# A gated delta rule with U times values and U times keys made ahead of the chunk scan

## The chip, the cores and the metric

One core of a Trainium2 chip runs the whole kernel. The metric is the device time of one execution in microseconds (us). Each core has five engines that run their own instruction lists in order and wait for each other by semaphores: TensorE (PE in the profile; its weight loads are PEld), VectorE (DVE), ScalarE (ACT), GpSimd (POOL) and SyncE (SP), whose list is a queue of DMA transfers. PSUM is the memory that TensorE writes, in banks of 128 partitions by 512 float32.

## The reference

One block of a decoder: 1024 tokens of width 1024 are normalised and projected; two mixers run side by side, each output is gated and projected up, the two are merged by sigmoid gates, and an output projection, a residual add and a last normalisation follow. Mixer A is a dilated window attention. Mixer B, which the change touches, is a gated delta rule with 8 heads of 64 keys by 64 values, computed in 16 chunks of 64 tokens:

```python
a = jnp.einsum('bhnid,bhnjd->bhnij', k_beta, kc) * decay_strict
t_inv = lax.linalg.triangular_solve(eye + a, ...)
u = t_inv @ (vc * bc[..., None])
w = t_inv @ (k_beta * jnp.exp(G)[..., None])
attn = jnp.einsum('bhnid,bhnjd->bhnij', qc, kc) * decay_incl
...
def step(state, inp):
    q_e, at, u_c, w_c, k_d, dec = inp
    v_new = u_c - jnp.einsum('bhck,bhkv->bhcv', w_c, state)
    o = jnp.einsum('bhck,bhkv->bhcv', q_e, state) + jnp.einsum('bhij,bhjv->bhiv', at, v_new)
    state = state * dec[..., None, None] + jnp.einsum('bhck,bhcv->bhkv', k_d, v_new)
    return state, o
```

`t_inv` (called U in the kernel, up to scalings by beta and by the norm of the keys) can be applied to values and keys for all chunks at once, as the reference does, or inside the scan to their difference, since u − w·S = t_inv·(beta·v − beta·exp(G)·(k·S)).

## The kernel before

Almost all of TensorE's time goes to projections. They are made in float16 with high and low parts: a *tick* is three matmuls of 128x512 (lines 171 to 173: high·high, high·low, low·high). A *unit* is 32 ticks, or 28 where a Strassen-like form with seven products is used; the 796 ticks of the units from the keys of mixer B on are handed out by an object called the Feed. TensorE's order is written by hand: the code of the mixers runs in program order, and wherever a step depends on another engine it calls `feed.tick(n)` to put n ticks of projection between; `feed.until(name)` runs ticks until a unit is done, and `feed.later(n, fn)` calls fn after n more ticks. The order on the other engines is made by a scheduler by priorities, and each engine, SyncE's queue too, then keeps that order. PSUM has tags of banks: three banks for projections, two each for G and S, one for O.

The order of the units is: the end of the attention's projections, then keys, values (two halves of four heads each), gates 3 and 4, queries, gate 5, z units a and b, gates 6 and 7, up-projections. Between them stand, in this order:

- `pg` (lines 1065 to 1076): sums of the log decays over chunks, by small matmuls from `gx` and `bg`, with exponentials on ScalarE; five ticks stand ahead of it, and the attention of its last set of heads runs behind it.
- `decay(hb)` for a half hb of the heads (lines 1126 to 1141): a tile `gm` is made on VectorE for each of 8 token tiles and multiplied by a mask of ones; two ticks are given to the first tile.
- `keys_side` (1190): sums of squares, k·k products (`pairs`, line 1181, 4 runs of 32 matmuls of 64x64, in all four quadrants of the array), and `spill_keys`, which multiplies keys from PSUM by a decay and writes `kd` to DRAM. `solve` (1221) inverts 32x32 blocks on VectorE.
- `values` (1299): after the conv of values, two `turn`s transpose them (line 1306), VectorE multiplies by beta into `rv`, and `rv` goes to DRAM. The second turn stands three ticks behind the first.
- `merge(hb)` (1246): joins the 32x32 blocks to U by `left` and `right` (1265 and 1280), with five ticks between its three stages; U is then written to DRAM.
- `pairs(hb, qT, ...)`: the masked q·k products, written to DRAM.

The chunk scan (from line 1454) goes over 8 token tiles of two chunks each. A chunk has three runs of dependent matmuls of 64x64, each float32 matmul showing as two instructions in the trace:

1. k·S and q·S (line 1485, 16 matmuls). VectorE makes z = rv − bgk·(k·S) by two multiplies of 128x128 and two subtractions of 64x256. Ticks: 4.
2. U·z (line 1506, 8 matmuls). VectorE multiplies by rk to `vn`. Ticks: 2.
3. kdec·vn (line 1515, 8 matmuls). VectorE adds to the state S (`Sb`). Ticks: 2.

After the two chunks of a tile comes at·vn (line 1526, 16 matmuls). The tick counts are PACE = (4, 2, 2).

Of the kernel before, what the change touches and what calls it, by code (L numbers as in the profile page):

```python
# [10 lines left out]
F32 = mybir.dt.float32  # L11
# [7 lines left out]
S = 1024  # L19
# [34 lines left out]
PACE = (4, 2, 2)  # L54
# [12 lines left out]
def hybrid_block(ctx: ExitStack, tc: tile.TileContext, A):  # L67
# [991 lines left out]
    feed.tick(5)  # L1059
    pg = bank("G", 2)  # L1060
# [3 lines left out]
    for h2 in range(2):  # L1064
        PE.matmul(pg[64 * h2:64 * h2 + 64, 128:192], lhsT=ones[:, 0:64],
                  rhs=gx.rearrange("p t c (q e) -> p (t c) q e", e=2)[:, :, :, h2],
                  start=True, stop=True, skip_group_check=True)
# [5 lines left out]
    SC.copy(hi4, pg[:, 192:256].rearrange("p (a t h) -> p a t h", a=2, t=8))
    ggf = gg.rearrange("p t h -> p (t h)")
    PE.matmul(pg[:, 0:64], lhsT=upto, rhs=ggf, start=False, stop=True, skip_group_check=True)
# [651 lines left out]
```

## Time and profile before

| | us |
|---|---|
| runs | 1113.74, 1116.79, 1113.9 |
| median | 1113.9 |
| the profiled execution | 1113.02 |
| its span | 1111.2 |
| TensorE busy | 1069.2 |
| VectorE busy | 843.8 |
| ScalarE busy | 545.6 |
| the scan lies between about | 790 and 912 |

The span runs from the first instruction to the last; 1.8 us lie around it. A row of a group of instructions gives line, engine, operation, output and inputs by name, size, count, then busy time and the mean in ns of one, then the idle time of the engine just before such instructions with the engine and line that ended it. Rows of the timeline give a start, a duration and the instructions joined in it. Matmuls overlap: the step from one start to the next tells what one costs, not its duration.

### The profile page before, as it was taken

To read this page: it belongs to the slowest core of one execution; us is meant where nothing else is said; L and a number is where in the kernel's file an instruction comes from. 1 tells how busy PE (TensorE), PEld (TensorE's weight loads), DVE (VectorE), ACT (ScalarE), POOL (GpSimd) and SP (SyncE) were. 2 spreads that over 40 slices of the span, in tenths; PEclk is the share of its full clock that TensorE was granted. 3 is DMA by queue.
4 is the path that set the end of the run, shared out by engine and by line. 5 is a ranking of instruction groups with operands and counts; after the bars stand their busy time and mean duration, and the time that the engine had idled before them with its cause. 6 is when DMAs were issued, how large, how long until landed. Compare 5 with 4: busy or idle time off the path is not lost.

```text
span 1111.2 us, 23274 instructions
## 1 busy us (share of the span) xinstructions
PE 1069.2 (96%) x9230; PEld 646.3 (58%) x9230; DVE 843.8 (76%) x1970; ACT 545.6 (49%) x1218; POOL 57.5 (5%) x103
## 2 busy tenths in 40 slices
PE   6999999999999999989989999999999999999997
PEld 6894685765957755856545544455455554444444
DVE  5798988879879689969955996975788777775223
ACT  6455766666666656457634523243543345331211
POOL 1200000000000000000010000000000000110000
PEclk9999999999999999999999999999999999999999
DMA  8144522623517233631234346373654444662221
GB/s 288 58 109 120 135 75 68 167 66 114 127 49 179 80 101 90 168 102 45 72 106 125 116 128 176 108 211 142 195 163 120 123 153 147 243 206 77 78 95 57
DMA packets 91709, 138.33 MB, mean 124 GB/s; under 512 B 30784, under 2 KB 57792, under 8 KB 90704
## 3 DMA queue, kind: packets, MB, share of 16 engines
q1 hardware_dynamic: 70368, 86.12, 26.3%
q0 software_dynamic: 12128, 44.11, 12.7%
q10 hardware_dynamic: 9104, 6.62, 1.9%
q8 instruction: 72, 1.18, 0.5%
q14 instruction: 37, 0.30, 0.1%
HBM read 85.24 MB, written 32.70 MB: 106 GB/s over the span
## 4 chain that ended last, share of the span: by engine, by line
PE 55%; DVE 30%; ACT 8%; issue 3%; DMA 3%; SPq 0%; ACTq 0%; DVEq 0%
PE ps_mm L171 14%; PE ps_mm L173 14%; PE ps_mm L172 14%; DVE rt L75 3%; DVE wlo L72 3%; ACT sm L770 2%; DVE ca L72 2%; DVE tl L75 2%; DVE sm L766 2%; DVE ro L75 2%; DVE pcAl L75 1%; PE ps_S L172 1%; PE ps_S L171 1%; PE ps_S L173 1%; DVE pcBl L75 1%
## 5 line engine op out<-in xcount | busy, mean ns | idle before, releaser
L173 PE MATMUL ps_mm<-h_hi,wlo 128*128 128x512 f16 (+1 forms) x552 | 208.8, 378 | 0.8 <-DVE wlo L72 0.8
L172 PE MATMUL ps_mm<-h_lo,whi 128*128 128x512 f16 (+1 forms) x492 | 186.0, 378 | 0.8 <-DVE h_lo L75 0.8
L171 PE MATMUL ps_mm<-h_hi,whi 128*128 128x512 f16 (+1 forms) x492 | 186.5, 379 | 0.0
L173 PEld LDWEIGHTS <-wlo 128*128 128x128 f16 x788 | 77.4, 98 | 89.4 <-issue 2.7
L172 PEld LDWEIGHTS <-whi 128*128 128x128 f16 x848 | 83.3, 98 | 70.5 <-issue 5.8
L171 PEld LDWEIGHTS <-whi 128*128 128x128 f16 x848 | 83.2, 98 | 69.9 <-issue 1.1
L171 PE MATMUL ps_mm<-whi,h_hi 128*128 128x256 f16 x384 | 105.1, 274 | 0.0
L173 PE MATMUL ps_mm<-whi,h_lo 128*128 128x256 f16 x384 | 104.7, 273 | 0.0
L172 PE MATMUL ps_mm<-wlo,h_hi 128*128 128x256 f16 x384 | 104.7, 273 | 0.0
L770 ACT ACTIVATE sm<-sm,osb 128x128 f32<-128x128 f32 (+1 forms) x160 | 69.6, 436 | 56.7 <-DVE osb L766 53.6
L72 DVE SCALAR_TENSOR_TENSOR wlo<-wstage,whi 128x1024 f16<-128x1024 f32 x50 | 60.9, 1219 | 13.4 <-ACT whi L154 13.2
L75 DVE TENSOR_TENSOR tl<-ps_G,th 128x256 f16<-128x256 f32 (+1 forms) x96 | 51.9, 541 | 20.9 <-ACT th L785 20.8
L766 DVE CUSTOM_DVE_ANT_0 sm<-ps_S,amask 128x128 f32<-128x128 f32 (+1 forms) x192 | 59.2, 346 | 8.3 <-PE ps_S L759 8.2
L75 DVE TENSOR_TENSOR rt<-rx,tabs 128x512 f32<-128x512 f32 x96 | 64.4, 686 | 1.4 <-ACT rx L576 0.4
L72 DVE SCALAR_TENSOR_TENSOR ca<-xc,cw,ca 128x512 f32<-128x512 f32 x72 | 53.6, 745 | 4.5 <-ACT ca L992 3.6
L780 PE MATMUL ps_G<-cons,sm 128*128 128x128 f32 x280 | 48.4, 276 | 4.9 <-ACT sm L770 2.3
L154 ACT ACTIVATE whi<-wstage 128x1024 f16<-128x1024 f32 x49 | 51.5, 1051 | 0.9 <-DMA wstage<-in_w 0.8
L171 PE MATMUL ps_mm<-wo,mhi 128*128 128x512 f16 (+2 forms) x136 | 49.5, 366 | 0.0
L172 PE MATMUL ps_mm<-wo,mhi 128*128 128x512 f16 (+2 forms) x136 | 49.5, 366 | 0.0
L173 PE MATMUL ps_mm<-wo,mlo 128*128 128x512 f16 (+2 forms) x136 | 49.4, 366 | 0.0
L780 PEld LDWEIGHTS ps_G<-cons,sm 128*128 128x128 f32 x280 | 35.5, 141 | 22.4 <-ACT sm L770 6.0
L172 PEld LDWEIGHTS <-h_hi 128*128 128x128 f16 x384 | 45.8, 119 | 1.7
(324 smaller groups left out, 2526.2 us busy)
## 6 DMA issues: line engine op xcount, KB each, us to landing
wstage<-in_w POOLq DMA_DIRECT2D x68, 512.0 KB, 5.0
og<-osb ACTq DMA_DIRECT2D x32, 132.0 KB, 2.3
og<-og SPq DMA_DIRECT2D x32, 132.0 KB, 2.2
gspa<-gst SPq DMA_DIRECT2D x16, 256.0 KB, 2.0
gspb<-gst SPq DMA_DIRECT2D x16, 256.0 KB, 3.3
sga<-gspa SPq DMA_DIRECT2D x8, 512.0 KB, 5.1
wstage<-in_w_up POOLq DMA_DIRECT2D x8, 512.0 KB, 5.1
sgb<-gspb SPq DMA_DIRECT2D x8, 512.0 KB, 5.9
```

The source lines that it names most:

```text
L72: (eng or V).scalar_tensor_tensor(out, in0, scalar, in1, op0=op0, op1=op1)
L75: (eng or V).tensor_tensor(out, in0, in1, op)
L154: in_turn(SC.activation(hi[:, 4 * c:4 * c + 4], st, AF.Copy, scale=W_SCALE))
L171: PE.matmul(out, lhsT=wh(k), rhs=mh(k), start=first and i == 0, stop=False, skip_group_check=True)
L172: PE.matmul(out, lhsT=wh(k), rhs=ml(k), start=False, stop=False, skip_group_check=True)
L173: last_pe[0] = PE.matmul(out, lhsT=wl(k), rhs=mh(k), start=False, stop=last and i == len(ks) - 1, skip_group_check=True).ins.name
L766: V.tensor_tensor_reduce(P[:, u, :128 * nk], psc[:, u * 256:u * 256 + 128 * nk], mask, -cexp, -NEG, ALU.add, ALU.min, accum_out=osb[:, 256 ...
L770: SC.activation(P[:, u, :128 * nk], P[:, u, :128 * nk], AF.Exp, bias=osb[:, 256 + hd:257 + hd], scale=-1.0, accum_out=osb[:, 260 + hd:261 ...
L780: PE.transpose(pt[:, c:c + 128], P[:, u, i * 128:i * 128 + 128], ident)
```

## The change

- A new generator `state_parts(hb)` runs ten ticks (`UW_LAG[1]`) after `merge(hb)`: for each group of four token tiles it reads `rv` and the keys times beta and decay (`kb`) back from DRAM, makes u = U·rv and w = kb·U by 64 matmuls of 64x64 (a batch) into two G and two S banks, has ScalarE copy the four banks into tiles `uw` (tag rv, three buffers) and writes them to DRAM by six transfers. Between the two batches of a half stand 14 ticks in half 0 (`UW_LAG[0] + UW_LAG[2]`) and 6 in half 1.
- The scan reads u, w, q, kd and at from DRAM and has two runs a chunk: w·S and q·S, with two subtractions vn = u − w·S of 128x128 behind it, and kdec·vn. Ticks: PACE = (3, 3). The loads of U and rv in the scan, the multiply by rk and the scaling by bgk are gone; beta and rk are folded into U by one multiply of 128x1024 in `solve`.
- `keep_keys` has ScalarE copy the keys from PSUM, and `spill_keys`, now after `pairs`, makes kd and kb of them by two multiplies of 128x1024 a group and writes both to DRAM.
- `pg` with its matmuls is put into `over_chunks`, which `feed.later` calls after 20 ticks; the five ticks ahead of it are gone. The first two `gm` tiles take the place of a tile `x7`. The second turn of values stands six ticks behind the first. Gate 6 goes ahead of the z units, behind gate 5.
- DRAM tensors between stages: kd, rv, kb, u, w, a and q (2 MB each, written and read), where there were kd, rv, U, a and q.

```diff
-PACE = (4, 2, 2)
+PACE = (3, 3)
+UW_LAG = (8, 10, 6)
...
-AT = 1
+V_GAP = 6
+GM_LAG = 2
+PG_LAG = 20
+PAIR_TICKS = 4
...
-    feed.tick(5)
-    pg = bank("G", 2)
...
+    def over_chunks():
+        pg = bank("G", 2)
...
+    feed.later(PG_LAG, over_chunks)
     feed.tick(ATT_LEAD)
     feed.run(att_run(*sets[-1], tiles[sets[-1]], ATT_PACE_LAST))
...
-            gm = p2_.tile([128, 2, 2, 64], F32, name="gm", tag="gm", bufs=2)
+            if hb == 0 and t < 2:
+                if t == 0:
+                    room = wst.tile([128, 512], F32, name="x7", tag="x7", bufs=1)
+                gm = room[:, 256 * t:256 * t + 256].rearrange("p (e q i) -> p e q i", e=2, q=2)
+            else:
+                gm = p2_.tile([128, 2, 2, 64], F32, name="gm", tag="gm", bufs=2)
...
+    def spill_keys(hb):
+        hs = slice(4 * hb, 4 * hb + 4)
+        for g in range(2):
+            ts = slice(4 * g, 4 * g + 4)
+            k = key_rows(hb, g)
+            kd = p2_.tile([128, 4, 4, 64], F32, name="kd", tag="T1p", bufs=1)
+            TT(kd, k, bc(eGl[:, ts, hs], 64), ALU.mult)
+            nc.sync.dma_start(out=kd_d[ts, :, hs].rearrange("t p h c -> p t h c"), in_=kd)
+            TT(k, k, bc(bgk[:, ts, hs], 64), ALU.mult)
+            nc.sync.dma_start(out=kb_d[hb][:, ts], in_=k)
...
+        TT(X, X, bsc[:, 1, None, :].to_broadcast([128, 32, 32]), ALU.mult)
...
+    def state_parts(hb):
+        def load(g):
+            ts = slice(4 * g, 4 * g + 4)
+            rv = p2_.tile([128, 4, 4, 64], F32, name="rvt", tag="vT", bufs=2)
+            tag = ("As", "X")[g] if hb else "vT"
+            kb = p2_.tile([128, 4, 4, 64], F32, name="kbt", tag=tag, bufs=1 if hb else 2)
+            nc.sync.dma_start(out=rv, in_=rv_d[ts, :, 4 * hb:4 * hb + 4].rearrange("t p h v -> p t h v"))
+            nc.sync.dma_start(out=kb, in_=kb_d[hb][:, ts])
+            return rv, kb
+        loads = [load(g) for g in range(1 + hb)]
+        yield
+        for g in range(2):
+            if g and not hb:
+                loads.append(load(g))
+                feed.tick(UW_LAG[0])
+            rv, kb = loads[g]
+            pu, pw = [[bank(n, 2), bank(n, 2)] for n in "GS"]
+            for n in range(8):
...
+                            PE.matmul(pu[r][b:b + 64, o:o + 64], lhsT=Ub, rhs=rv[rs, t, 2 * q + e], ...)
...
+                            PE.matmul(pw[r][b:b + 64, o:o + 64], lhsT=kb[rs, t, 2 * q + e], rhs=Ub, ...)
+            for x, ps2 in enumerate((pu, pw)):
+                for r in range(2):
+                    uw = p2_.tile([128, 4, 2, 64], F32, name="uw", tag="rv", bufs=3)
+                    with tc.high_priority():
+                        SC.copy(uw, ps2[r].rearrange("p (t q i) -> p t q i", q=2, i=64))
...
+            yield
...
-            feed.later(V_LAG + 3, lambda: turn(4))
+            feed.later(V_LAG + V_GAP, lambda: turn(4))
...
+    def state_side(hb):
+        parts = state_parts(hb)
+        next(parts)
+        merge(hb, *solved[hb], packs[hb])
+        feed.tick(UW_LAG[1])
+        for _ in parts:
+            feed.tick(UW_LAG[2])
...
-                with tc.high_priority():
-                    for e in range(2):
-                        TT(z[:, e::2], hv(pkq[e][:, :128]), bc(bv[:, e::2], 64), ALU.mult)
-                    for hb in range(2):
-                        r = rows(c2 ^ hb)
-                        TT(z[r], rvt[r, 4 * hb:4 * hb + 4], z[r], ALU.subtract)
+                        TT(vn[:, c2, e], un[:, c2, e], hv(pwq[e][:, :128]), ALU.subtract)
...
-            pvn = bank("O", 1)
-            for n, (hb, j) in enumerate(order):
-                PE.matmul(pvn[r, j * 64:j * 64 + 64], lhsT=U[r, hb, j % 2, j // 2], rhs=z[r, j], ...)
-            with tc.high_priority():
-                TT(vn[:, c2], hv(pvn[:, :256]), bc(rks[:, t, c2], 64), ALU.mult)
-            feed.tick(PACE[1])
```

Three places show how the instructions stand. The first is SyncE's queue around the merging of half 0. Before, the last `rv` is written and then U (u_d0) goes out:

```order
L1312 DMA rv_d_8145<-rv_9461 128x4x128 [waits DMAHW2_49,DVE_49]
L1418 DMA u_d0_8147<-MT0_8136 128x1024 [waits DMAHW5_49,DMAHW3_49,Activation_49]
L1418 DMA u_d0_8147<-MT0_8136 128x1024 [waits DMAHW4_49,Activation_49]
L912 DMA gspb1_9597<-gst_9598 128x512 [waits Activation_49]
L912 DMA gspb1_9597<-gst_9626 128x512 [waits DMAHW6_49,Activation_49]
L1242 DMA u_d1_9087<-X_8989 128x1024 [waits DMAHW7_49,DVE_49,Pool_49]
```

After, the loads for the second batch (rvt, kbt) stand around the six writes of the first:

```order
L916 DMA gspb1_9600<-gst_9629 128x512 [waits DMAHW6_49,Activation_49]
L1328 DMA rvt_9737<-rv_d_8126 128x4x256 [waits DMAHW7_49,PE_49]
L1365 DMA un_d_8130<-uw_9700 64x4x128 [waits DMAHW0_49,Activation_49]
L1365 DMA un_d_8130<-uw_9700 64x4x128 [waits DMAHW1_49]
L1365 DMA un_d_8130<-uw_9704 64x4x128 [waits DMAHW2_49,Activation_49]
L1365 DMA un_d_8130<-uw_9704 64x4x128 [waits DMAHW3_49]
L1362 DMA wn_d_8131<-uw_9708 128x4x128 [waits DMAHW4_49,Activation_49]
L1362 DMA wn_d_8131<-uw_9711 128x4x128 [waits DMAHW5_49,Activation_49]
L1329 DMA kbt_9738<-kb_d0_8132 128x1024 [waits DMAHW6_49,PE_49]
```

The writes of U are gone from the queue, and the second load of keys is its seventh transfer after the load of values.

The second place is ScalarE behind the merging of half 1. Before, its two last copies into U (MT1) are followed by a gate's eviction (gst), a scaling of squares in PSUM and a weight piece:

```order
L1287 COPY MT1_8138<-ps_O_10185 32x16x32 [waits PE_49]
L1287 COPY MT1_8138<-ps_O_10185 32x16x32
L911 ACTIVATE gst_10317<-ps_mm_10178 128x512 [waits DMAHW6_49,PE_49,Activation_49]
L1167 ACTIVATE ps_S_10329<-ps_S_10329 128x512 [waits PE_49]
L318 ACTIVATE whi_10349<-wstage_10074 128x512 [waits DMASW1_49]
```

After, the evictions of the batches stand there, four for the first batch, and the first of the second:

```order
L322 ACTIVATE whi_10515<-wstage_10253 128x512 [waits DVE_49]
L1360 COPY uw_10501<-ps_G_10433 128x512 [waits DMAHW5_49,PE_49]
L1360 COPY uw_10505<-ps_G_10434 128x512 [waits DMAHW3_49,DMAHW2_49,PE_49]
L1360 COPY uw_10509<-ps_S_10435 128x512 [waits DMAHW4_49,PE_49]
L915 ACTIVATE gst_10534<-ps_mm_10420 128x512 [waits DMAHW2_49,PE_49,Activation_49]
L1360 COPY uw_10512<-ps_S_10436 128x512 [waits DMAHW4_49,DMAHW3_49,Activation_49]
L1360 COPY uw_10612<-ps_G_10544 128x512 [waits DMAHW5_49,DMAHW6_49,PE_49,Activation_49]
```

A gate's eviction stands ahead of the fourth, and the copies wait for DMA queues, the writes of tiles that had the same buffers.

The third place is TensorE behind the last projection of gates, at the sums over chunks. Before, after a transposing product of the attention's outputs (osb) a last tick comes, and then `pg`:

```order
L866 MATMUL ps_G<-cons,osb 128x128 x2
L171 LDWEIGHTS whi
L171 MATMUL ps_mm<-h_hi,whi 128x512
L172 LDWEIGHTS whi
L172 MATMUL ps_mm<-h_lo,whi 128x512
L173 LDWEIGHTS wlo
L173 MATMUL ps_mm<-h_hi,wlo 128x512
L1065 MATMUL ps_G<-gx,cons 64x64 x2
L1071 MATMUL ps_G<-bg,cons 64x64 x2
L1075 MATMUL ps_G<-bg,cons 128x64
L1076 MATMUL ps_G<-bg,cons 128x64
```

After, the scores of the last attention set (Ks by Qh and Ql) follow there:

```order
L870 MATMUL ps_G<-cons,osb 128x128 x2
L761 LDWEIGHTS Qh
L761 MATMUL ps_S<-Ks,Qh 128x128
L763 LDWEIGHTS Ql
L763 MATMUL ps_S<-Ks,Ql 128x128
```

The four rows of `pg` now come sixteen ticks later, between ticks, as L1070, L1076, L1080 and L1081.

More of the change, by code (lines that the diff above doesn't have):

```diff
@@ L1435, in hybrid_block @@
         pairs(hb, qT, E[hb])
-        spill(1, hb, E)
+        spill(hb)
         sumsq(hb, qT, rq[:, :, 4 * hb:4 * hb + 4])
-    feed.until(("gate", 5))
+    feed.until(("gate", 6))
     gctx.close()
@@ L1457, in hybrid_block @@
             by_chunk(rqs, rq)
-        rvt = cp.tile([128, 8, 64], F32, name="rvt", tag="rvt", bufs=2)
-        nc.sync.dma_start(out=rvt, in_=rv_d[t])
-        U = cp.tile([128, 2, 2, 2, 64], F32, name="U", tag="U", bufs=2)
-        at = cp.tile([128, 2, 2, 2, 64], F32, name="at", tag="at", bufs=AT)
+        un = cp.tile([128, 2, 2, 2, 64], F32, name="un", tag="un", bufs=2)
+        wt = cp.tile([128, 2, 4, 64], F32, name="wt", tag="wt", bufs=2)
+        at = cp.tile([128, 2, 2, 2, 64], F32, name="at", tag="at", bufs=2)
@@ L1473, in hybrid_block @@
[L1473 removed]
+        vn = cp.tile([128, 2, 2, 2, 64], F32, name="vn", tag="vn", bufs=2)
         for c2 in range(2):
             ch = 2 * t + c2
[L1476 removed]
+            ov = ob[:, t, 4 * c2:4 * c2 + 4]
             if ch:
[L1479 removed]
+                pwq = [bank("S", 2), bank("S", 2)]
                 for i in range(2):
[L1481 to L1487 removed]
+                    for q in range(2):
+                        for e, hb in ((0, 0), (1, 1), (0, 1), (1, 0)):
+                            b, c, o = c2 ^ hb, 2 * hb + q, (2 * i + q) * 64
+                            src = qt[rows(e), c, b] if i else wt[rows(e), c2, c]
+                            PE.matmul(pwq[e][rows(b), o:o + 64], lhsT=src, rhs=Sb[rows(e), c],
+                                      start=(i == 0 and q == 0), stop=True, skip_group_check=True)
@@ L1496, in hybrid_block @@
                 TT(Sb, Sb, bc(dec[:, t, c2], 64), ALU.mult)
             else:
-                GP.memset(oq[:, 0], 0.0)
+                GP.memset(ov, 0.0)
                 feed.tick(SCAN_LEAD)
-                for hb in range(2):
-                    SC.copy(z[rows(hb)], rvt[rows(hb), 4 * hb:4 * hb + 4])
+                SC.copy(vn[:, 0], un[:, 0])
             feed.tick(PACE[0])
-            pvn = bank("O", 1)
-            for n, (hb, j) in enumerate(order):
-                r = rows(c2 ^ hb)
-                PE.matmul(pvn[r, j * 64:j * 64 + 64], lhsT=U[r, hb, j % 2, j // 2], rhs=z[r, j],
-                          start=(n < 2), stop=True, skip_group_check=True)
@@ L1514, in hybrid_block @@
                     r, c = rows(c2 ^ hb), 2 * hb + q
-                    PE.matmul(pS[hb][rows(e), q * 64:q * 64 + 64], lhsT=kdec[r, 2 * c + e], rhs=vn[r, c2, 2 * q + e],
+                    PE.matmul(pS[hb][rows(e), q * 64:q * 64 + 64], lhsT=kdec[r, 2 * c + e], rhs=vn[r, c2, e, q],
                               start=(q == 0), stop=True, skip_group_check=True)
@@ L1520, in hybrid_block @@
                     TT(sv, sv, hv(pS[hb][:, :128]), ALU.add)
-            feed.tick(PACE[2])
+            feed.tick(PACE[1])
         po = bank("G", 2)
@@ L1564, in hybrid_block @@
             feed.tick(2)
-    feed.until(("gate", 6))
+    feed.until(("z", "b", 1))
     feed.tick(1)
```

139 lines of the change are left out of this document (73 added, 66 removed).

## The prediction

> **What bounds the kernel now.** I read the page first, for the engine that sets the end.
>
> ```profile
> PE 1069.2 (96%) x9230; PEld 646.3 (58%) x9230; DVE 843.8 (76%) x1970; ACT 545.6 (49%) x1218; POOL 57.5 (5%) x103
> ...
> PE   6999999999999999989989999999999999999997
> ...
> PEclk9999999999999999999999999999999999999999
> ...
> PE 55%; DVE 30%; ACT 8%; issue 3%; DMA 3%; SPq 0%; ACTq 0%; DVEq 0%
> ```
>
> TensorE is busy 96% of the span, the granted clock is near full, and the idle slices lie where the delta-rule part is prepared (slices 17, 20). So a change is worth what it takes from TensorE's own list plus TensorE's waits; another engine counts only where TensorE waits for it. Next come the waits, from the groups of TensorE instructions between 430 and 912 us (last column: idle time just before, with its releaser).
>
> ```profile
> L1506 PE MATMUL ps_O<-z,U 64*64 64x64 f32 x256 | 12.0, 225 | 0.5 <-DVE z L75 0.4
> L1306 PE MATMUL ps_O<-cons,vT 128*128 128x128 f32 x32 | 4.9, 275 | 3.7 <-DVE rv L75 3.7
> L1280 PE MATMUL ps_O<-MT,Y 32*32 32x32 f32 x256 | 5.0, 192 | 2.3 <-DVE rv L75 2.3
> L1135 PE MATMUL ps_G<-gm,cons 128*128 128x256 f32 x32 | 9.6, 382 | 1.5 <-DVE gm L75 1.5
> L1075 PE MATMUL ps_G<-bg,cons 128*128 128x64 f32 x2 | 0.4, 299 | 0.6 <-ACT bg L1073 0.6
> L1065 PE MATMUL ps_G<-gx,cons 128*64 128x64 f32 x4 | 0.3, 240 | 1.9 <-issue 1.9
> ```
>
> The chunk scan itself (U·z, L1506) waits only 0.5 us in all its sixteen chunks: its chain of dependent steps is already covered by projection work. The long waits stand ahead of it: 1.9 at the sums of gates, 1.5 at the first decay tile, 3.7 at the transposes of values, 2.3 in the merging. Then the windows, for what those waits do to the clock (columns: window, its length, busy of PE, PEld, DVE, ACT, POOL, granted clock, DMA share, GB/s).
>
> ```profile
> 485.00:490.00 5.00, 3.90 (x20) 1.72 (x17) 4.67 (x12) 4.54 (x10) 0.53 (x1) 1.00 0.19 51
> 490.00:495.00 5.00, 3.64 (x20) 1.89 (x21) 3.10 (x9) 3.15 (x7) 0.00 (x0) 0.79 0.23 81
> 495.00:500.00 5.00, 5.00 (x28) 2.52 (x27) 3.12 (x12) 2.84 (x10) 0.53 (x1) 0.87 0.31 105
> ...
> 675.00:680.00 5.00, 3.15 (x18) 1.66 (x17) 3.16 (x6) 2.61 (x8) 0.00 (x0) 1.00 0.43 94
> ...
> 695.00:700.00 5.00, 3.95 (x134) 2.24 (x135) 4.63 (x14) 1.15 (x2) 0.09 (x1) 0.77 0.66 211
> 700.00:705.00 5.00, 5.00 (x80) 2.59 (x79) 4.55 (x14) 1.18 (x3) 0.00 (x0) 0.89 0.14 57
> ...
> 790.00:912.00 122.00, 121.04 (x1626) 63.63 (x1625) 98.32 (x243) 47.70 (x80) 4.22 (x8) 1.00 0.46 145
> ```
>
> Two waits are followed by a stretch of lowered clock: 0.79 and 0.87 after the sums of gates, 0.77 and 0.89 after the merging. Each costs 5×0.21 + 5×0.13 = 1.7 us, or 5×0.23 + 5×0.11 = 1.7. The wait of 1.85 in 675 to 680 had none (1.00). The scan (790 to 912) has VectorE at 98.3 of 122 us.
>
> **The change part by part.** First TensorE's list. A run of small matmuls costs the gap that it makes in the row of 512-wide ones.
>
> ```profile
> 822.48 0.38 PE L173 MATMUL ps_mm<-h_hi,wlo 128*128 128x512 f16 x1
> 822.78 0.68 PE L1506 MATMUL ps_O<-z,U 64*64 64x64 f32 x16
> 823.40 0.39 PE L171 MATMUL ps_mm<-h_hi,wlo 128*128 128x512 f16 x1
> ...
> 824.49 0.38 PE L173 MATMUL ps_mm<-h_hi,wlo 128*128 128x512 f16 x1
> 824.80 0.46 PE L1515 MATMUL ps_G<-vn,kdec 64*64 64x64 f32 x16
> 825.19 0.39 PE L171 MATMUL ps_mm<-sum4h,whi 128*128 128x512 f16 x1
> ...
> 736.88 0.38 PE L173 MATMUL ps_mm<-h_hi,wlo 128*128 128x512 f16 x1
> 737.19 1.16 PE L1181 MATMUL ps_G<-qT,kT 64*64 64x64 f32 x64
> 738.28 0.39 PE L171 MATMUL ps_mm<-h_hi,whi 128*128 128x512 f16 x1
> ```
>
> Neighbours start 0.216 us apart (from 824.49 to 825.19 with the run between, less that step). So U·z costs 823.40 − 822.48 − 0.216 = 0.70 us, the kdec run 0.48, a run of 32 matmuls in all four quadrants 738.28 − 736.88 − 0.216 = 1.18. (A float32 matmul is two rows of the trace: x16 is 8 matmuls.) Removed: 16 × 0.70 = 11.2. Added: state_parts, four batches of 64 matmuls in four quadrants, each twice 1.18 = 2.4 at most, and 2.1 if the fixed part (from 8 matmuls at 0.48 to 32 at 1.18: 0.029 each, 0.25 fixed) is paid once; 2.2 taken, 8.8 in all (8.4 to 9.4). At the two-quadrant price of U·z it would be 8 × 0.70 = 5.6 a batch; that is a rival. **Net −2.4.** So the third run of the scan comes back almost whole as batches; w·S replaces K·S with the same count.
>
> The sums of gates leave their place behind five ticks of feed (a tick is three matmuls, 3 × 0.216 = 0.65 us) and come sixteen ticks later, when gx and bg are long there: **−1.9** (the 0.57 for bg stays), and the lowered clock behind it **−1.7** (0 if another wait falls there). The first two decay tiles get a place that waits for no transfer: **−1.2** of 1.5 (0 to −1.5).
>
> The second transposes of values come six ticks behind the first in place of three. Waited for there: VectorE's rv, 1.82 and 1.85 us, and 2.35 in the merging, 6.0 in all; three ticks are 1.94 us, about the size of each wait. But in the new order the last transposes of the first half stand two ticks ahead of right(), and VectorE is full then: I keep 2.0 of it, **−4.0** (0 to −6.0). With the 2.35 gone or shortened, the lowered clock behind it goes too, **−1.7** (0 to −1.7).
>
> New waits. The second batch of state_parts stands 14 ticks behind the first for half 0 and 6 ticks for half 1.
>
> ```profile
> L1287 ACT COPY MT<-ps_O 32x512 f32<-32x512 f32 x6 | 3.5, 576 | 6.9 <-PE ps_O L1280 6.8
> ...
> rv_d<-rv SPq DMA_DIRECT2D x8, 256.0 KB, 3.6
> ...
> As<-m_d SPq DMA_DIRECT2D x2, 512.0 KB, 4.5
> ```
>
> An ACT eviction of a bank takes 0.58; a 256 KB write landed after 3.6 us and a 512 KB read after 4.5. In half 0 the keys of the second batch (kbt) are issued in SyncE's queue behind six writes; the last of these waits for the fourth eviction, and that for one of three uw buffers, free when the first write has landed: 2.2 + 0.58 + 3.6 + 0.58 = 7.0 us after the batch starts, up to 9 with the issues between; landed 11.5 to 13.5. TensorE arrives after 2.2 + 14 × 0.65 = 11.3: **+2.0** (0 to +4). Queued behind kbt are only the gate's spills; behind the batch stands all of TensorE's feed. In half 1 all four loads are early, but the fourth eviction again waits for the first write, 7.0, and for a gate's eviction of the same size (0.6) ahead of it in ACT's queue, 7.6, while TensorE wants the bank at 2.2 + 6 × 0.65 = 6.1: **+1.5** (0 to +2.5). One of the two may bring its own stretch of low clock: **+1.7** (0 to +3.4).
>
> By the Trainium skill ("TensorE: Matmul & The Clock Gate", Part 1) the clock falls after an idle window of about 3.4 us. The waits of 1.9 with 0.57 behind it and of 2.35 brought stretches of low clock, so here less was enough and the rows decide; each lost 1.7, half of the page's window. By the page neither new wait would lower the clock, and an estimate by its figure would be 1.7 lower than mine.
>
> The scan. A chunk goes from 8 ticks and three runs to 6 ticks and two; its steps get 3 ticks = 1.94 us each.
>
> ```profile
> L75 DVE TENSOR_TENSOR z<-rvt,z 64x256 f32<-64x256 f32 x30 | 12.5, 418 | 0.7
> ...
> L75 DVE TENSOR_TENSOR Sb<-Sb,ps_G 128x128 f32<-128x128 f32 x32 | 7.7, 279 | 6.9 <-PE ps_G L1515 6.9
> L75 DVE TENSOR_TENSOR z<-ps_S,bgks 128x128 f32<-128x128 f32 x30 | 7.2, 281 | 1.6 <-PE ps_S L1485 1.5
> L75 DVE TENSOR_TENSOR vn<-ps_O,rks 128x256 f32<-128x256 f32 x16 | 6.7, 417 | 3.5 <-PE ps_O L1506 3.4
> L317 DVE TENSOR_TENSOR wstage<-wstage 128x512 f32<-128x512 f32 x18 | 12.3, 681 | 0.1
> L72 DVE SCALAR_TENSOR_TENSOR whi<-wstage,whi 128x512 f16<-128x512 f32 x18 | 12.2, 684 | 2.5 <-ACT whi L318 2.5
> L72 DVE SCALAR_TENSOR_TENSOR wlo<-wstage,wlo 128x512 f16<-128x512 f32 x14 | 9.4, 683 | 1.0 <-ACT wlo L318 1.0
> ```
>
> Before, two multiplies and two subtractions (2 × 0.28 + 2 × 0.42 = 1.40) fitted into four ticks (2.59), the multiply of vn into two (1.29), and the two adds of 0.28 into two, with 0.8 us of waits in all sixteen chunks (0.5 in the row of L1506, 0.3 at L1515). Now two subtractions of 0.28 stand in 1.94 and the two adds in 1.94: looser. VectorE's own work falls by 12.5 + 7.2 + 6.7 = 26.4 us and grows by 30 × 0.28 = 8.4; the weight pieces (12.3 + 12.2 + 9.4 = 33.9) fall by the quarter of the ticks that moves out, 8.5. So 98.3 becomes 71.8, in a scan shorter by 32 ticks (20.7) and the U·z runs (11.2), 90.1: 80%, about as full as before (81%). The feed holds 796 runs of three matmuls in both kernels, so those 32 ticks come behind the scan and cost nothing new. I put **+0.4** for steps that now stand closer together (0 to +1.0).
>
> Costed at nothing: VectorE's added work ahead of the first solve.
>
> ```profile
> 670.92 2.24 SPq L1253 DMA_DIRECT2D T1p<-t_d  x1
> ...
> 691.90 1.22 DVE L75 TENSOR_TENSOR As<-As,bsc 128x1024 f32<-128x1024 f32 x1 [0.42 <-DMA As<-m_d]
> ...
> 688.11 1.20 PE L1265 MATMUL ps_S<-T1p,MT 32*32 32x32 f32 x64
> ```
>
> Eight 128x1024 multiplies of keys at 1.22 (9.8) replace eight of 128x512 at the 0.68 of the weight pieces (5.4), for both halves, and the solve gets one of 1.22. The attention ahead starts five ticks (3.2 us) earlier, so the first solve comes about as before. Its last result was requested at 670.92 and first used at 688.11: with 4.5 for landing there are over 10 us of cover. Without it each us late is one of wait at left(). The extra 8 MB of transfers are hidden in the same way, except those costed above; gate 6 moved forward is the same matmuls at another place (±1 at the tail).
>
> The sum: −2.4 − 1.9 − 1.7 − 1.2 − 4.0 − 1.7 + 2.0 + 1.5 + 1.7 + 0.4 = −7.3. The profiled execution took 1113.0 (its span 1111.2, and 1.8 around it), so 1105.7; the median of the runs is 0.9 above it, 1113.9, so **1106.6**. The terms do not all come to one end together: the transposes at −6.0, kbt at 0 and half 1 at +1.0 give 4.5 less, 1102; kbt at +4 and the low clock at +3.4 give 3.7 more, 1110.3. **Its own range: 1102 to 1110.5.**
>
> **The rivals.** (a) No change that can be told (I call 0.3%, 3.3 us, the least that can be). The gains at the transposes stay away, because VectorE, not the distance, is late there: −4.0 and −1.7 become 0, and the sum is −1.6: 1112.3. For it: VectorE is at 4.6 of 5.0 us around the merging (695 to 705). Against it: in 675 to 680 it was at 3.16, so there it was order and not load.
>
> The Trainium skill ("TensorEngine Tiling (Array Packing)", Performance Considerations, PSUM Bottleneck) speaks against the change in this direction: packed matmuls make the emptying of PSUM the bound, and it advises two engines for it, where the new batches use ACT alone. Four evictions of 0.58 make 2.3 against 2.2 of matmuls, so an estimate by that rule alone gives no wait after six ticks.
>
> (b) Slower, by the scan: with two fewer ticks the projection's weight pieces on VectorE (0.68 each) fall more often ahead of a step of the chain. One ahead gives 0.56 + 0.68 = 1.24 of 1.94, no wait; two give 1.92 and with the way between engines about 0.35 of wait. If that happens at both steps in each of 15 chunks it is 15 × 0.7 = 10.5: 1117.1. It decides from two pieces a step on. For it: VectorE as full as before. Against it: the tighter windows before led to 0.8 us of waits in sixteen chunks. (c) Slower, by the batches: at 5.6 us each they cost 22.4 and not 8.8, +13.6: 1120.2. For it: the same 64x64 shape as U·z. Against it: the pairs run has the same four quadrants as the batches, and 1.18 for 32.
>
> **How the numbers follow.** Forecast 0.68 (0.65 of it faster, 0.03 within the bound), (a) 0.18, (b) 0.08 (0.06 slower, 0.02 within), (c) 0.06. So faster 0.65, same 0.23, slower 0.12. The time is the forecast's, 1106.6. The range takes the forecast's ends two us further down (all waits absent) and (a) above: 1100 to 1113.5.
>
> **What would show it.** State_parts' rows of about 2.2 us each, no row like L1506; the sums of gates without the 1.9 and the clock at 1.00 around them; under 2.5 us of waits for rv in place of 6.0; a wait for a DMA of about 2 at the third quarter of a half's parts, and one on ACT's uw of about 1.5 in half 1; in the scan no wait on vn or Sb above 0.2 a chunk. It is wrong if the new waits exceed 6 us together, if the scan waits more than 3, or if the waits for rv stay.

## The result

The changed kernel took 1119.57 us (median of 13 runs, 1115.07 to 1123.43), the kernel before, now in 13 runs, 1116.41. The ratio is 1.0035 with a 95% interval of 1.0018 to 1.0052: **slower by 0.35%**, some 4 us, where 0.66% faster was forecast (1106.6, range 1100.0 to 1113.5). The profiled execution has a span of 1116.1 against 1111.2. TensorE and its windows after the change (first row of the page, then length, busy time of PE, PEld, DVE, ACT, POOL, granted clock, DMA share, GB/s):

```profile
PE 1067.5 (96%) x9486; PEld 647.6 (58%) x9486; DVE 829.8 (74%) x1918; ACT 556.6 (50%) x1241; POOL 57.2 (5%) x103
```

```profile
570.00:710.00 140.00, 136.22 (x1258) 72.85 (x1257) 105.75 (x211) 57.45 (x99) 7.75 (x15) 1.00 0.52 151
710.00:790.00 80.00, 76.45 (x1121) 41.39 (x1120) 46.01 (x84) 34.68 (x63) 2.11 (x4) 0.98 0.65 190
790.00:930.00 140.00, 131.94 (x1550) 67.55 (x1548) 103.23 (x243) 63.37 (x105) 6.65 (x13) 0.99 0.51 161
```

The same windows of the kernel before:

```profile
570.00:710.00 140.00, 132.46 (x1117) 70.48 (x1116) 102.45 (x217) 51.50 (x89) 7.75 (x15) 0.99 0.45 129
710.00:790.00 80.00, 80.00 (x861) 41.55 (x859) 55.07 (x103) 36.44 (x63) 3.48 (x7) 1.00 0.53 168
790.00:930.00 140.00, 137.72 (x1730) 71.12 (x1728) 115.05 (x275) 58.33 (x96) 5.28 (x10) 1.00 0.44 139
```

What TensorE is not busy is waiting. From 570 to 710 (decay, transposes, merging) it falls from 7.5 to 3.8 us; the forecast had 5.2 less (1.2 at the decay tile, 4.0 at rv), but 1.2 came up at the k·k products (MT) and 1.0 in the merging. From 710 to 790 (batches, q·k) it rises from 0 to 3.6, and from 790 to 930 (scan) from 2.3 to 8.1. The waits by what ended them, from 430 to 915 us of the change (total, times, longest):

```profile
PE ps_mm L175 <- ACT gst L915: 2.8, 1, 2.8
PE ps_G L1203 <- DVE E L79: 2.6, 3, 2.0
...
PE ps_mm L177 <- DVE wlo L76: 1.6, 1, 1.6
PE ps_O L1376 <- DVE rv L79: 1.5, 1, 1.5
...
PE ps_G L1577 <- DVE ob L79: 1.3, 1, 1.3
PE ps_S L1559 <- DVE Sb L79: 1.3, 2, 0.8
PE ps_G L1203 <- DVE MT L79: 1.2, 2, 1.0
...
PE ps_S L1353 <- DMA kbt<-kb_d: 0.8, 1, 0.8
PE ps_G L1080 <- ACT bg L1078: 0.6, 1, 0.6
PE ps_S L1353 <- ACT uw L1360: 0.5, 1, 0.5
PE ps_G L1577 <- DVE vn L79: 0.4, 1, 0.4
```

The waits at the batches (kbt, uw) are 1.3 in all, less than forecast. The two largest of all stand where the prediction had none: at a gate's eviction when the scan begins (gst, 2.8) and at the q·k products (E, of which the longest is 2.0). Both are followed by low clock:

```profile
740.00:745.00 5.00, 3.00 (x66) 2.26 (x67) 4.13 (x8) 1.67 (x3) 0.53 (x1) 0.71 1.04 262
745.00:750.00 5.00, 5.00 (x27) 2.75 (x26) 3.00 (x6) 1.96 (x4) 0.00 (x0) 0.95 1.06 304
815.00:820.00 5.00, 3.36 (x10) 1.23 (x10) 1.63 (x3) 1.60 (x3) 1.06 (x2) 0.72 0.87 276
820.00:825.00 5.00, 5.00 (x66) 2.41 (x65) 0.64 (x3) 1.33 (x3) 0.00 (x0) 0.94 0.34 135
835.00:840.00 5.00, 4.18 (x61) 2.14 (x58) 5.00 (x14) 2.68 (x5) 0.00 (x0) 1.00 0.25 71
840.00:845.00 5.00, 5.00 (x88) 2.93 (x81) 5.00 (x12) 2.61 (x6) 0.00 (x0) 1.00 0.91 271
```

5 × (0.29 + 0.05) and 5 × (0.28 + 0.06) are 1.7 us each, as in the kernel before: two stretches there, two here, at other places. The last two rows show VectorE full (5.00 of 5.00) in the scan's early chunks.

TensorE's own work came out as worked out. The first batch stands between these two matmuls:

```profile
703.05 0.38 PE L177 MATMUL ps_mm<-h_hi,wlo 128*128 128x512 f16 x1
705.39 0.39 PE L175 MATMUL ps_mm<-h_hi,whi 128*128 128x512 f16 x1
```

705.39 − 703.05 − 0.22 = 2.12 us; the third batch takes as much, the other two wait besides. Four times 2.12 is 8.5, for the 11.2 of U·z: −2.7.

**Time at full clock.** Every run of a kernel carries its span and mean granted clock (to three digits, so 0.6 us either way in one run). Span × (1 − clock) is the column "low clock", the rest of the span, work and waits, is "full clock"; both are means over the runs, and "median" is the device time. Medians and means leave out the few runs, one of uw4 and some of the kernel before, that were over 1.5% longer than the fastest. The column holds some low clock that costs nothing: TensorE is done about 6 us before the span ends, and its clock falls there too, by 0.2 us (before) to 2.0 us (uw4, keys_pool) in the 17 profiles, 1.3 on average. So both columns are good to about 1 us. uw_alone has 4 runs, before_edits, un_direct and edits_pair6 have 6, evict_both (not in the table) has one, the others 11 or more.

| kernel | median | ratio to before (95%) | full clock | low clock |
|---|---|---|---|---|
| before (in four sessions) | 1114.1 to 1115.5 | 1 | 1108.4 to 1109.0 | 4.1 to 4.9 |
| the change | 1119.57 | 1.0035 (1.0018 to 1.0052) | 1113.9 | 4.0 |
| before_edits | 1110.41 | 0.9953 (0.9940 to 0.9965) | 1105.1 | 3.3 |
| uw_alone | 1129.9 | 1.0134 (1.0119 to 1.0149) | 1120.2 | 8.5 |
| gap6 | 1114.72 | 1.0006 (0.9992 to 1.0020) | 1107.1 | 5.9 |
| pg_late | 1115.35 | 1.0005 (0.9994 to 1.0017) | 1109.1 | 3.8 |
| gm_room | 1112.32 | 0.9977 (0.9965 to 0.9989) | 1107.7 | 3.2 |
| gst3 | 1117.82 | 1.0021 (1.0009 to 1.0034) | 1112.5 | 3.4 |
| un_direct | 1120.49 | 1.0049 (1.0035 to 1.0063) | 1114.1 | 4.9 |
| pair6 | 1116.7 | 1.0001 (0.9988 to 1.0014) | 1110.6 | 3.6 |
| uw4 | 1115.36 | 1.0008 (0.9991 to 1.0026) | 1110.1 | 3.7 |
| repaired | 1113.28 | 0.9981 (0.9970 to 0.9992) | 1106.6 | 4.8 |
| repaired4 | 1111.41 | 0.9981 (0.9969 to 0.9993) | 1107.7 | 2.3 |
| keys_pool | 1115.9 | 1.0005 (0.9991 to 1.0020) | 1110.1 | 4.2 |
| z_pool | 1112.27 | 0.9973 (0.9962 to 0.9984) | 1106.7 | 4.1 |
| edits_pair6 | 1108.88 | 0.9938 (0.9922 to 0.9954) | 1105.0 | 1.7 |

The slowdown is at full clock: 4.9 us over before's 1109.0 (5.5 over the lowest of its sessions; its clocks in the change's own session are not on record). Low clock takes no more than before.

### The profile page after: what moved, and what is told of

It reads as the page before. It is cut to its first block, busy times and chain, and to the rows that moved or that the text cites. A ratio compares the mean times of both kernels' runs of the same rounds, so it can differ in the third digit from the quotient of the medians.

```text
span 1116.1 us, 23809 instructions
## 1 busy us (share of the span) xinstructions
PE 1067.5 (96%) x9486; PEld 647.6 (58%) x9486; DVE 829.8 (74%) x1918; ACT 556.6 (50%) x1241; POOL 57.2 (5%) x103
## 5 line engine op out<-in xcount | busy, mean ns | idle before, releaser
L76 DVE SCALAR_TENSOR_TENSOR whi<-wstage,whi 128x512 f16<-128x512 f32 x60 | 40.6, 686 | 16.3 <-ACT whi L322 15.5
```

Source lines behind the costliest of these rows:

```text
L76: (eng or V).scalar_tensor_tensor(out, in0, scalar, in1, op0=op0, op1=op1)
```

## The experiments

**Which part loses: the u, w form or the edits beside it?** The change mixes the two. The three edits are the later sums of gates, the other place of the first two gm tiles, and the six ticks between the turns of values. before_edits puts only these on the kernel before, uw_alone takes them out of the change. What is called the u, w form below is all the rest of the change: the batches, the shorter scan, the multiplies of keys, and gate 6 ahead of the z units. No run here puts gate 6 back alone.

```diff
 # before_edits (on before); uw_alone is the reverse (on the change)
-    feed.tick(5)
-    pg = bank("G", 2)
+    feed.later(PG_LAG, over_chunks)
...
-            gm = p2_.tile([128, 2, 2, 64], F32, name="gm", tag="gm", bufs=2)
+            if hb == 0 and t < 2: gm = room[:, 256 * t:256 * t + 256] ...
...
-            feed.later(V_LAG + 3, lambda: turn(4))
+            feed.later(V_LAG + V_GAP, lambda: turn(4))
```

> The kernel before with only the three edits beside the u, w form: the sums of gates delayed by 20 ticks, the first two gm tiles in another place, the second turn of values six ticks behind the first. Theory (the gains that the trace of the change shows at these places, 1.9 + 1.5 + 4.6 = 8.0 us of waits, are real and belong to these edits): about 8 us faster than before, ratio 0.992 to 0.994, with no wait of 1.9 at the sums, none at the first decay tile and under 2 us for rv. Rival (the waits come back at the next place, because VectorE or ScalarE is late there anyway): within 2 us of before, ratio 0.998 to 1.002.

> The change without those three edits (sums of gates in their old place, gm in its old tile, second turn three ticks behind the first): the u, w form alone. Theory: it costs what the change costs and the 8 us of gains on top, ratio to before about 1.010 (1127 where before has 1116). Rival (the edits gave nothing here): ratio about 1.0035, like the change.

Measured 0.9953 and 1.0134. The edits gain 5 us on the kernel before, not 8, and 11 on the u, w form (1.0134 to 1.0035). The u, w form loses 9 us with them and 15 without (1.0134); at full clock 8.8 (1113.9 against 1105.1) and 11.2 (1120.2 against 1109.0). In the profile of uw_alone a wait of 5.6 us stands at the q·k products, and low clock takes 8.5 a run. The theory's direction holds, its sizes don't add.

**Why 5 and not 8.** Each edit alone, on the kernel before.

```diff
 # gap6
-            feed.later(V_LAG + 3, lambda: turn(4))
+            feed.later(V_LAG + 6, lambda: turn(4))
 # pg_late: only the feed.later(PG_LAG, over_chunks); gm_room: only the gm tiles
```

> The kernel before with one edit: the second turn of values six ticks behind the first. The prediction's term: 4.0 us of waits and 1.7 of low clock, 5.7 in all, ratio 0.995. Rival (VectorE is late and the wait moves to the merging, or was not in the timed runs): within 1.5 us of before, 0.9985 to 1.0015.

> The kernel before with one edit: the sums of gates delayed by 20 ticks, with the five ticks ahead of them gone. The prediction's term: 1.9 us of wait and 1.7 of low clock, 3.6 in all, ratio 0.9968. Rival (the wait and the low clock come back a few microseconds away, at the attention of the last set, which now starts earlier): within 1.5 us of before, 0.9985 to 1.0015.

> The kernel before with one edit: the first two gm tiles of half 0 in the place of the tile x7. The prediction's term: 1.5 us of wait at the first decay tile less, no change of the clock, ratio 0.9986. Rival (this is the edit that carries the gain of the three, 5 us, since the other two alone gave nothing): ratio 0.995 to 0.9965.

gap6 gave 1.0006, pg_late 1.0005, gm_room 0.9977. TensorE's waits in gap6, 430 to 930 us:

```profile
PE ps_G L1181 <- DVE E L75: 2.8, 1, 2.8
PE ps_mm L173 <- DVE wlo L72: 2.5, 1, 2.5
...
PE ps_O L1306 <- DVE rv L75: 1.7, 1, 1.7
...
PE ps_O L1280 <- DVE rv L75: 0.4, 1, 0.4
```

The waits for rv fell from 6.0 to 2.1, just the 4.0 of the prediction, and 2.8 came up at the q·k products, where the kernel before had none. VectorE's emptying of those banks (E) stands right behind three convolution steps (ca), first in the kernel before, then in gap6 with TensorE's first run:

```profile
737.36 2.32 DVE L72 SCALAR_TENSOR_TENSOR ca<-xc,cw,ca 128x512 f32<-128x512 f32 x3
```

```profile
732.26 1.16 PE L1181 MATMUL ps_G<-qT,kT 64*64 64x64 f32 x64
...
735.97 2.32 DVE L72 SCALAR_TENSOR_TENSOR ca<-xc,cw,ca 128x512 f32<-128x512 f32 x3
```

TensorE's first run of these products comes 4.9 us sooner (732.26 for 737.19), VectorE's steps only 1.4, so TensorE waits. Low clock now stands behind that wait, in windows that had 1.00 before:

```profile
735.00:740.00 5.00, 2.00 (x24) 0.99 (x25) 4.42 (x8) 2.45 (x5) 0.53 (x1) 0.90 1.04 230
740.00:745.00 5.00, 5.00 (x75) 3.15 (x68) 2.82 (x4) 1.18 (x2) 0.53 (x1) 0.76 0.87 234
```

In pg_late, in the view of waits:

```profile
PE ps_mm L174 <- DVE wlo L73: 2.9, 1, 2.9
PE ps_O L1283 <- DVE rv L76: 2.6, 1, 2.6
PE ps_O L1309 <- DVE rv L76: 2.0, 1, 2.0
...
PE ps_G L781 <- ACT sm L771: 1.6, 1, 1.6
...
PE ps_G L1184 <- DVE MT L76: 1.3, 2, 1.0
```

The 1.9 is gone, and 1.6 (0.5 before) stands at a step of the attention that now starts earlier (L781) and 1.3 at the k·k products. The wait for a weight piece near 478 us (wlo) was 0.8 in the profile of before and 1.1 to 2.9 in the others, with the same code there; so single profiles differ by 2 us and by a stretch of clock. gm_room's gain is 2.6 us, more than the 1.5 forecast, although 1.4 came up at q·k; only 1.1 of it is at full clock (1107.7 against 1108.8 in its session), and its profile has no stretch of low clock. In the other direction gap6 is 1.3 faster at full clock (1107.1 against 1108.4) and loses that to low clock (5.9 against 4.1). At full clock the three together make 3.9 (1105.1 against 1109.0), where alone they make 1.1 (gm_room), 1.3 (gap6) and −0.7 (pg_late): the gains need each other. For gap6 the rows show why, the next late step; for the other two it is likely but not shown.

**The gate's eviction at the start of the scan.** gst3 gives the gates' evictions a third buffer, un_direct takes away ScalarE's copy of un to vn.

```diff
 # gst3
-            gpool[:] = fp, "gst", 2
+            gpool[:] = fp, "gst", 3
 # un_direct
-                SC.copy(vn[:, 0], un[:, 0])
+            vs = vn if ch else un
... (kdec·vn reads vs, and the first at·vn reads un)
```

> The change with three buffers in place of two for the gates' evictions from the end of the preparation on. In the change TensorE waits 2.8 us at 816.6 for ScalarE's eviction of gate 6, and that waits for the write of an earlier buffer; a stretch of low clock (3.4 us at half) follows. Theory (the transfer's round trip is what it waits for): that wait goes, 2.8 us and with the clock up to 4.5 less than the change, ratio to before 0.9995 to 1.001. Rival (ScalarE itself is late, because its copy of un waits for a load at 809.6): under 1 us less, ratio 1.003.

> The change with the first chunk's vn read from un itself: ScalarE's copy of un to vn at the start of the scan is gone. In the change, and with three gst buffers too, this copy holds ScalarE for 3.1 to 3.3 us until the load of un has landed (809.6), and the evictions of gate 6 stand behind it. Theory: this copy is what makes the eviction late, so TensorE's wait of 2.8 us for gst falls below 1 and the time by 2 to 4.5 us (with a stretch of low clock): ratio to before 0.9995 to 1.0015. Rival (only the transfers of gst are late): under 1 us, ratio 1.003.

In the change ScalarE shows both waits:

```profile
809.63 0.40 ACT L1571 COPY vn<-un 128x256 f32<-128x256 f32 x1 [3.12 <-DMA un<-un_d]
...
816.00 0.60 ACT L915 ACTIVATE gst<-ps_mm 128x512 f32<-128x512 f32 x1 [1.38 <-DMA gspb<-gst]
```

gst3 gave 1.0021, un_direct 1.0049; neither is told apart from the change (1.0018 to 1.0052). TensorE's wait is 1.5 in the one and 2.3 in the other, but it is also 1.3 in uw4, 2.2 in pair6 and 3.0 in evict_both below, which leave this place as it is; so its size alone proves nothing. ScalarE, first in gst3 and then in un_direct:

```profile
807.72 0.40 ACT L1571 COPY vn<-un 128x256 f32<-128x256 f32 x1 [3.25 <-DMA un<-un_d]
```

```profile
814.80 0.63 ACT L915 ACTIVATE gst<-gst 128x512 f32<-128x512 f32 x1 [2.48 <-DVE gst L76]
...
818.76 0.60 ACT L915 ACTIVATE gst<-ps_mm 128x512 f32<-128x512 f32 x1 [2.01 <-DMA gspb<-gst]
```

Either cause can hold the eviction by itself: the copy that waits for a load, or the buffers that wait for their writes (VectorE's step on gst, for which ScalarE waits 2.48, itself waits 2.0 for such a write). Taking one away leaves the other; so un_direct's theory fell, and gst3's holds at most in part. In repaired and the three kernels built on it, with both away and other repairs beside, the wait is gone.

**Distance at the pairs, the ring of uw, two evicting engines.**

```diff
 # pair6
-PAIR_TICKS = 4
+PAIR_TICKS = 6
 # uw4: last is a tile of 128x1024 in the place of T1p
+                    if x and r:
+                        uw = last[:, 512 * g:512 * g + 512]...
 # evict_both
-                        SC.copy(uw, ps2[r]...)
+                        (V.tensor_copy if r else SC.copy)(uw, ps2[r]...)
```

> The change with six ticks in place of four behind each run of the k.k and q.k products. In the change the second run waits for VectorE to empty the banks, 2.3 us in all for q.k and 1.2 for k.k, with a stretch of low clock behind the first. Theory (distance was too short): 3 to 5 us less than the change, ratio to before 0.999 to 1.001. Rival (VectorE's list has longer work ahead of these evictions and the wait moves along): within 1 us of the change, ratio about 1.003.

> The change with the fourth eviction of each batch going to a tile of its own, so that it doesn't wait for the write of the first. In the change that copy waits 3.6 and 4.3 us on ScalarE in half 0 (9.9 us in all four batches), with the evictions of the query convolutions queued behind it; VectorE's convolution steps and then its emptying of the q.k banks come late, and TensorE waits 2.0 there and 1.3 at the batches. Theory (this ring holds ScalarE, and with it the rest): ScalarE's waits for writes of un fall from 9.9 to under 4, TensorE's waits at the batches below 0.5 and at q.k below 1, 2 to 4 us less than the change, ratio to before 0.9995 to 1.002. Rival (ScalarE has slack there, the q.k wait of 1.9 is in the three edits without any u, w form as well): within 1.5 us of the change, ratio 1.002 to 1.005.

> The change with one bank of each pair of the batches evicted by VectorE and one by ScalarE (all four by ScalarE in the change). Theory (evictions bound nothing here, the writes and the load of keys do): the waits at the batches stay at 0.8 for the load and at most 0.5 for uw, the span within 2 us of the change's 1116.1. Rival (the emptying of the banks by one engine is what holds the batches): the waits at the batches go below 0.3 in all, and ScalarE's later work comes earlier, 2 us or more less.

pair6 gave 1.0001, within the theory: the waits at k·k are gone and E is 1.2. uw4 gave 1.0008, also the theory's band. What it takes away is on ScalarE, here the change:

```profile
706.35 0.60 ACT L1360 COPY uw<-ps_S 128x512 f32<-128x512 f32 x1
710.52 0.59 ACT L1360 COPY uw<-ps_S 128x512 f32<-128x512 f32 x1 [3.56 <-DMA un_d<-uw]
...
721.33 0.60 ACT L1360 COPY uw<-ps_S 128x512 f32<-128x512 f32 x1
...
727.27 0.59 ACT L1360 COPY uw<-ps_S 128x512 f32<-128x512 f32 x1 [4.27 <-DMA un_d<-uw]
727.75 0.63 ACT L1007 ACTIVATE qT<-ca 128x512 f32<-128x512 f32 x1
```

The fourth copy of a batch waits 3.6 and 4.3 us for the first one's write, and a query convolution stands behind it. In uw4 these waits for un are gone from ScalarE, and TensorE's wait for uw with them; but its waits at q·k (1.6) and for kbt (1.0) did not fall as expected. By the ratio uw4 is not told apart from the change, at full clock it is 3.8 lower (1110.1 against 1113.9; the kernel before is 0.6 lower in that session too); how the gain reaches TensorE is not shown. One part of why kbt stays late shows in SyncE's queue, first in the change and then in uw4:

```profile
706.00 3.07 SPq L1365 DMA_DIRECT2D un_d<-uw  x4
709.17 2.33 SPq L1362 DMA_DIRECT2D wn_d<-uw  x2
711.59 0.46 SPq L1329 DMA_DIRECT2D kbt<-kb_d  x1
```

```profile
710.87 0.71 SPq L1329 DMA_DIRECT2D kbt<-kb_d  x1
```

The issues of the six writes ahead of it take from 706.0 to 711.5. Without the ring's wait kbt goes out only 0.7 sooner, and then lands after 5.3 us in place of 4.0; why it lands later is not shown.

evict_both, with a single run, has a span of 1115.9 and waits of 2.2 for kbt and 0.3 for uw at the batches: the emptying by one engine was not what held them. The Trainium skill ("TensorEngine Tiling (Array Packing)", PSUM Bottleneck) says that the emptying may become the bottleneck of packed matmuls and advises two engines; the wait of that kind is small in this trace, 0.5 with one engine and 0.3 with two. The wait for E at q·k fell from 2.6 to 0.8, but not because ScalarE's later work came earlier: E itself comes 1.2 later (742.2 for 741.0), and TensorE, held for kbt, 3.0 later (738.84 for 735.86).

**All repairs, and the old form with the same distance.**

```diff
 # repaired: un_direct + gst3 + pair6, and
-UW_LAG = (8, 10, 6)
+UW_LAG = (11, 10, 7)
 # repaired4: repaired + uw4;  edits_pair6: before_edits, and in pairs
-            feed.tick(4)
+            feed.tick(6)
```

> The change with all repairs at once: un read directly, three gst buffers, six ticks behind each run of pairs, and 3 and 1 ticks more around the batches (UW_LAG 11, 10, 7). Theory (the u, w form loses by waits at these four places, 2.8 + 2.3 + 1.2 + 1.3 us and the clock behind them, and can be mended there): 7 to 9 us less than the change, ratio to before 0.994 to 0.997, about the three edits alone. Rival (a wait taken away comes back at the next place, since the same work of VectorE and ScalarE has to be done before the scan): 2 to 4 us less than the change, ratio 0.999 to 1.002.

> The kernel before with the three edits and six ticks behind each run of pairs, without the u, w form. In the three edits alone TensorE waits 2.2 us at the q.k products and 1.2 at the k.k products, as in the change. Theory: these waits belong to the order that the edits make and go with the distance: 2 to 3 us less than the three edits, ratio to before 0.992 to 0.994. Rival (VectorE is late there anyway): as the three edits, 0.995 to 0.996.

> All repairs at once, and the fourth eviction in a tile of its own. Theory: the wait of 2.5 us at q.k and the stretch of low clock behind it go, 2 to 4 us less than all repairs (0.9981), ratio to before 0.9945 to 0.9965, level with the old form with the same distances (0.9938). Rival: as all repairs, 0.9975 to 0.9985, and the u, w form stays 4 to 5 us behind the old one.

repaired gave 0.9981: 7 us of the 9 that the u, w form loses at full clock come back (1113.9 to 1106.6, the edits alone have 1105.1). By the ratio neither band was met; it lies a little outside the rival's. repaired4 gave no more (0.9981, the rival's), though its profile has the q·k wait down to 1.3: a new wait of 1.5 came with it (T1p, whose place the fourth tile takes). edits_pair6, **the fastest kernel here, is 0.9938**, at the upper end of its theory; its interval overlaps with that of before_edits, so the distance alone is not shown to gain, and at full clock the two are level (1105.0 and 1105.1). The old form stays 0.4% ahead of the repaired new one. At full clock that is 1.6 us for repaired and 2.7 for repaired4; the rest is low clock.

**What is left.** keys_pool and z_pool put VectorE work of repaired4 on GpSimd.

```diff
 # keys_pool
-            TT(kd, k, bc(eGl[:, ts, hs], 64), ALU.mult)
+            TT(kd, k, bc(eGl[:, ts, hs], 64), ALU.mult, GP)
-            TT(k, k, bc(bgk[:, ts, hs], 64), ALU.mult)
+            TT(k, k, bc(bgk[:, ts, hs], 64), ALU.mult, GP)
 # z_pool
-        TT(n[:, 1, ts], gate, n[:, 0, ts], ALU.subtract)
+        TT(n[:, 1, ts], gate, n[:, 0, ts], ALU.subtract, GP)
```

> All repairs and the fourth tile, with the eight multiplies of keys (128x1024, 1.2 us each on VectorE) moved to GpSimd. Theory (what the u, w form still loses is VectorE's added work ahead of the merging: waits of 1.4 for rv, 1.1 and 1.5 at the merging, 0.7 for kss, and the 1.4 at q.k): those waits fall by 2 us or more and the ratio to before goes from 0.9981 to 0.996 or less. Rival (VectorE's order, not its load, makes these waits; GpSimd is slower at it and the solve of the blocks gets its keys no later): ratio 0.997 to 0.999, with the waits as they were.

> All repairs and the fourth tile, with the subtraction that makes the low part of the gated attention output (128x512, eight times in the scan) moved from VectorE to GpSimd. Theory (in the six-tick chunks VectorE is full while the z units run, 5.0 of 5.0 us from 835 to 845 in the change, and these pieces stand ahead of the chain): the waits in the scan, 4.0 us in five places, fall below 2, ratio to before 0.9955 to 0.997. Rival (other pieces take their place, or GpSimd is late): scan waits of 3 to 5 us, ratio 0.9975 to 0.999.

keys_pool gave 1.0005: slower than repaired4 (the intervals just touch), with a wait of 3.0 for rv, so neither band was met. On GpSimd such a multiply took 2.0 us (1.2 on VectorE), so it doesn't test VectorE's load cleanly. z_pool gave 0.9973, between its two bands and not told apart from 0.9981; its scan waits are 2.8 for 4.0. In the profiles, TensorE's idle time from 570 to 930 us is 12.2 in repaired4 and 6.8 in edits_pair6. That is 5.4 more, against the 2.7 of work that the form saves, and fits the 2.7 between their full clocks. The rows name the places: 1.5 more in the scan's chain (4.0 against 2.5), 1.5 at T1p, 1.4 more for rv, 1.2 more at the transposes of the scan's output (ob, zb), 0.7 at the keys' sums (kss), and 1.0 less at a gate's eviction. What makes VectorE late at them is not settled.

## Why the prediction was wrong

The forecast split in two: the three edits with their low clock at −10.5 (−1.9 − 1.7 − 1.2 − 4.0 − 1.7) and the rest at +3.2 (−2.4 + 2.0 + 1.5 + 1.7 + 0.4). Measured, by the ratios of before_edits and of the change, they are about −5 and +9. Either miss alone would have left the change faster; together they turned the sign.

**The work of TensorE: right.** −2.4 forecast, −2.7 measured; rival (c), batches at 5.6 us, fell at 2.12.

**The sums of gates, the decay tile, the transposes (−1.9, −1.2, −4.0): right as rows of the trace, wrong as gains.** In the change these waits are down by 1.9, 1.5 and 4.5 (from 6.0 to 1.5). As time they were worth 0, 2.6 and 0 us alone and 5 together. The step that failed is the addition: "a wait removed is time gained" holds only up to the next step whose data isn't earlier too. The prediction did not ask what is late next behind the transposes; it was the q·k products, 2.8 us in gap6. Rival (a) had the outcome for this edit, but not the way: the waits for rv did go.

**The low clock (−1.7, −1.7, +1.7): not to be read from one trace.** The kernel before loses 4.1 to 4.9 us a run by the table, about 3 without the tail, so the two stretches of the profiled run are usual; the change loses 4.0. But a stretch did not belong to its wait: the same 1.9 and 0.6 at the sums of gates brought none in gap6 and gm_room.

**The new waits at the batches (+2.0, +1.5): right in kind, 0.8 and 0.5.** kbt was issued 8.2 us after the first batch began (711.59 and 703.36), where 7.0 to 9 was forecast. But only TensorE's own wait was priced. The wait of the fourth eviction for the ring was seen, with its 7 us; what stands behind it on ScalarE was not priced beyond the second batch's bank.

**The scan (+0.4) and gate 6 at nothing: the largest error.** From 790 to 930 the idle time is 8.1 against 2.3. Of this, 2.8 is gate 6, which was called "the same matmuls at another place (±1 at the tail)"; before, a gate's eviction cost 1.0 behind the scan. Its matmuls are the same, but its evictions now pass ScalarE and SyncE's queue while the scan's first loads and un's copy stand there. Another 2.9 is the chain itself (0.4 for vn, 1.3 for Sb, 1.3 for a bank that VectorE's sum of ob still holds) against 0.7, and 1.5 stands at the transposes of its output against 0.3. The chain's waits are in rival (b)'s place and at its engine, VectorE full at 5.00 of 5.00, but four and not thirty. That the fullness makes them is likely: with one piece of this work moved off VectorE they fell from 4.0 to 2.8 (z_pool against repaired4). Rival (b)'s own 0.35 a step counted a way between engines that no row shows: U·z started 0.06 behind z (806.54 + 0.42, then 807.02).

So the sign was lost by waits that were costed at nothing or nearly so (1.8 more at gst, 2.2 more in the chain, 1.2 more behind it) and by gains of 8 that were worth 5. The waits at the pairs (2.6 for E and 1.2 for MT) are no loss of the u, w form for the most part: before_edits has 1.9 and 1.2 there, and they are where the edits' gains went. These rows are not the whole of the 9: the profiled runs of the change and of before_edits are 5 apart at full clock, the means of all runs 8.8. Of the signs that the prediction set for being wrong, two were met: the new waits passed 6 us together (2.8, 2.6, 1.2 and 1.3), and the scan waited more than 3 with gst counted.

## What to carry to other kernels

A removed wait is worth what the next late step leaves of it: go along the engine that sets the end to the following two or three waits, and ask of each whether its data comes earlier too; try each edit alone and all together. Work that is moved has to be priced on every queue that it passes, its evictions and writes more than its matmuls. An eviction into a ring that is freed by a DMA holds its whole engine for the write's round trip (3.6 to 4.3 us here), and where two causes hold one wait, taking one away may show nothing.

## What the runs showed of the hardware

Waits of 2.0 and 0.3 (741.7), of 2.8 (816.6) and, before, of 1.9 and 0.6 (490.8) and of 2.35 (696.0) were each followed by low clock that cost 1.7 us; one of 1.5 at 678 was not. The Trainium skill ("TensorE: Matmul & The Clock Gate", Part 1) asks for an idle window of about 3.4 us; 1.7 agrees with one window of that length at half clock, but less than a window of idleness was enough here. The half clock shows behind 816.6, where matmuls that otherwise start 0.216 us apart start 0.43 apart from 817.4 to 820.4:

```profile
817.84 0.63 PE L176 MATMUL ps_mm<-sum1l,whi 128*128 128x512 f16 x1
818.26 0.63 PE L177 MATMUL ps_mm<-sum1h,whi 128*128 128x512 f16 x1
```

The length of a wait does not decide alone: in gm_room waits of 1.9 and 0.6, of 2.3 in the merging and of 2.4 for wlo brought no low clock. The 17 profiles have none to four such stretches ahead of the tail, uw_alone the most.

The same 64x64 float32 matmuls cost 0.033 us each in a batch of 64 over four quadrants (2.12), 0.060 in a run of 8 over four (0.48), and 0.088 in a run of 8 over two (0.70).
